# RWKV stage of a decoder layer on one core: TensorE's order laid down by a counted clock over generators, the 16x16 inverses started one half ahead

## The chip, the cores and the metric

One NeuronCore of a Trainium2 chip runs the whole program. The metric is the device time of one execution in microseconds; the time before is the median of three runs, 2283.53 us (2280.61 to 2289.46).

## What is computed

One decoder layer over 1024 tokens of width 1024, all in float32: token mixing (RWKV-7 time mixing, sparse attention and two sigmoid gates, from one input projection), then memory cross-attention, then a gated MLP with a width-3 convolution. The change lies in the RWKV part alone:

```python
def step(state, inp):
    r_t, w_t, k_t, v_t, a_t, b_t = inp
    sa = jnp.einsum('bhvk,bhk->bhv', state, a_t)
    state = (state * w_t[:, :, None, :] + sa[..., None] * b_t[:, :, None, :]
             + v_t[..., None] * k_t[:, :, None, :])
    return state, jnp.einsum('bhvk,bhk->bhv', state, r_t)
```

Eight heads of 64 channels each carry a 64x64 state over 1024 steps. `a` is minus the normalised key and `b` is that key times a learned rate, so each step erases along the key and writes anew.

## The kernel before, in words

The recurrence is computed in chunks of 64 steps. The stage handles **units**: a unit is a pair of heads (128 partitions) and one half of the sequence (512 steps, 8 chunks), and there are 8 of them. What follows is done for each unit by the generator `rwkv_half`, which stops at two `yield`s.

* **Operands.** Two small products of the low-rank projections (`pw`, `pa`, L564 and L566), decays by a scan (`CU`, L572) and exponentials, the key's norm (`inv_norm`: `vs` L540, then transposes `bc` L552), scaled keys `BH`, `KH`, `BB`, `KB`.
* **Couplings.** For each chunk the 64x64 products `gb` (L615) and `gk` (L621), masked to triangles by VectorE into `GB` (L616) and `AMR` (L625); transposes `tr` (L630) into `KS`, `SV`, `ZV`; the bonus term `pbo` (L597).
* **Substitution.** The strictly lower triangle `LT` (a half of `GB`) has to be inverted as 1 - L. Its 16x16 diagonal blocks go out to DRAM and back in another layout (`d1`, L653; `LB`, L655), VectorE inverts them in 30 short rows (L662, L663), GpSimd copies (L664), and they return through DRAM (`d2`, L665) into `DD` and `EE` by 16 DMAs on SP's queue (L674).
* **Inverse.** Five groups of small matmuls combine 16x16 blocks to 64x64: `q` (L680), `d` (L686), `e` (L693), `q` (L700), `e` (L708), each with a VectorE or ScalarE step behind it.
* **Recurrence.** Per chunk three matmuls that depend on one another: `x` (L719), copied to `XS` by VectorE (L721); `sa` (L723), copied to `SV` by VectorE and ScalarE (L724, L725); `z` (L728), added to the decayed state `ZV` by VectorE (L731).
* **Outputs.** `psy` from `AMR` and `ZV` (L735) and from `GB` and `SV` (L738), a group norm by `inv_norm`, scale and bonus, one DMA to `ya` (L749).

Beside the units there is wide work, 128x128 weights against 512 columns, three matmuls to a product (`mm3`, L193 to L195): the projections `prj` that feed the units (13 of them, 48 matmuls each), and the merge gates `gt`. The gates belong to no unit: 16 column blocks of 48 matmuls, 768 in all, made by the generator `gate_parts` one k step (three matmuls) at a time. They are due only when the branches are merged, far behind.

What sets the order of the work: the scheduler of the framework places each engine's instructions by the order in which the code names them and by a priority. The code names a unit's first part two units ahead (`pre`), the recurrence of a unit and the inverse of the next with high priority, and after that a chunk of gates (16 k steps) as often as `GATES1` says:

```python
for i in range(8):
    with tc.high_priority(offset=100000):
        next(its[i], None)
        if i < 7:
            next(its[i + 1])
    if i < 6:
        pre(i + 2)
    for _ in range(GATES1[i]):
        gate_chunk()
```

The attention stage that follows first issues `gate_chunk(GT)` (8 k steps), loads keys and values (`kld`, `vld` on GpSimd's queue, transposes `kT` L808), and then runs key blocks (`weights`, `values`; the first matmul of a block's values is L944). At each block `fill` takes about one step of the generator `fillers`: what is left of the gates, then the products of the merge (`mg`), the second part of which waits until the upper half of the attention is stored.

Of the kernel before, what the change touches and what calls it, by code (L numbers as in the profile page):

```python
# [18 lines left out]
P = 128  # L19
# [29 lines left out]
XQ = 3  # L49
LC, LS = (2, 2)  # L50
# [73 lines left out]
def layer_kernel(ctx: ExitStack, tc, I, out, cst):  # L124
# [384 lines left out]
    def k4(name, dt=F32):  # L509
        return rp.tile([P, NC8, 2, CH], dt, tag="k4", name=name, bufs=8)  # L510
# [25 lines left out]
    def inv_norm(sq, bank_, tile_, scale, eps):  # L536
# [12 lines left out]
        S.activation(w.rearrange("p (a d) -> p a d", d=64), rs[:, :, None].to_broadcast([P, 8, 64]), AF.Copy)  # L549
        ps = bank_("bc")  # L550
# [6 lines left out]
    def rwkv_half(hp, half, X):  # L557
        Xr, Xk, Xv = X
# [12 lines left out]
        r8 = lambda a: a.rearrange("p (c t) -> p c t", t=CH)  # L571
# [4 lines left out]
        S.activation(E3, E3, AF.Exp, scale=-DEC)  # L576

        TMP, KKN = e2("TMP"), e2("KKN")
        S.activation(TMP, Xk, AF.Square, scale=pc("rwkv_k_k", hp))
        ps = inv_norm(TMP, pss, ew, 64.0, None)  # L580
# [5 lines left out]
        V.tensor_tensor(BH, BH, E2, op=OP.mult)  # L586
        V.tensor_tensor(KH, KP, E2, op=OP.mult)
# [6 lines left out]
        TMP, BV = e2("TMP2"), ec("BV")  # L594
        V.scalar_tensor_tensor(TMP, Xr, pc("rwkv_r_k", hp), KP, op0=OP.mult, op1=OP.mult)
        ps = pss("pbo")
        PE.matmul(ps, ones, TMP, start=True, stop=True)  # L597
        V.scalar_tensor_tensor(BV, ps, 64.0, Xv, op0=OP.mult, op1=OP.mult)

        AMR = k8("AMR")  # L600
        for h, rw in enumerate(rows_h):
            V.scalar_tensor_tensor(AMR[rw, :, 0, h, :], r8(KKN[rw]), -1.0, r8(E3[rw]), op0=OP.mult, op1=OP.mult)
            V.tensor_tensor(AMR[rw, :, 1, h, :], r8(Xr[rw]), r8(ET[rw]), op=OP.mult)

        GB, KS, SV, ZV = k4("GB"), k4("KS"), k4("SV"), k4("ZV")
        zvs[hp, half] = ZV
        if half == 0:
            for h, rw in enumerate(rows_h):
                G.memset(ZV[rw, 0, h, :], 0.0)
        for j in range(2):  # L610
            ps = pss("gb").rearrange("p (c a t) -> p c a t", a=2, t=CH)
            for ci in range(4):
                c = 4 * j + ci
                for h, rw in enumerate(rows_h):
                    PE.matmul(ps[rw, ci], BH[rw, c * CH:(c + 1) * CH], AMR[rw, c, :, h, :], start=True, stop=True)  # L615
            V.tensor_tensor(GB[:, 4 * j:4 * j + 4].rearrange("p c a t -> p c (a t)"), ps.rearrange("p c a t -> p c (a t)"), bc(gmask, 4), op=OP.mult)  # L616
            ps = pss("gk").rearrange("p (c a t) -> p c a t", a=2, t=CH)
            for ci in range(4):
                c = 4 * j + ci
                for h, rw in enumerate(rows_h):  # L620
                    PE.matmul(ps[rows_h[1 - h], ci], KH[rw, c * CH:(c + 1) * CH], AMR[rw, c, :, h, :], start=True, stop=True)  # L621
            for h in range(2):
                rx = rows_h[1 - h]
                m = gmask[rx].rearrange("p (a t) -> p a t", a=2)[:, None].to_broadcast([64, 4, 2, CH])
                V.tensor_tensor(AMR[rx, 4 * j:4 * j + 4, :, h, :], ps[rx], m, op=OP.mult)  # L625

        for src, flip, dsts in ((BB, 0, (KS,)), (KB_, 1, (KS,)), (Xv, 1, (ZV, SV))):
            ps = pss("tr").rearrange("p (c n) -> p c n", n=P)
            for c in range(4):
                PE.transpose(ps[:, c, :], src[:, c * P:(c + 1) * P], ident)  # L630
            if src is Xv:

                mv = sm.tile([P, 4, 2], F32, name="vm", tag="vm", bufs=2)
                V.tensor_reduce(mv, ps.rearrange("p c (h d) -> p c h d", h=2), axis=AX.X, op=OP.add)
            for q, rq in enumerate(rows_h):
                for h in range(2):
                    ro = rows_h[1 - h] if flip else rows_h[h]
                    for dst in dsts:
                        o, i = dst[ro, q:NC8:2, h, :], ps[rq, :, h * 64:h * 64 + 64]
                        if src is Xv:  # L640
                            m = mv[rq, :, h][:, :, None].to_broadcast([64, 4, 64])
                            V.scalar_tensor_tensor(o, m, -1.0 / 64, i, op0=OP.mult, op1=OP.add)
                        else:
                            S.activation(o, i, AF.Copy)


        LT = GB[:, :, 0, :]
# [16 lines left out]
        G.tensor_copy(DB[:, 1], DB[:, 0].rearrange("p a b -> p b a"))  # L664
        SP.dma_start(d2.rearrange("w a c s t -> (a c) w (s t)"), DB.rearrange("p w s t -> p w (s t)"))  # L665
        UU, DD, EE = r8(et("UU")), r8(et("DD")), kd("EE")
        QQ = UU
        G.memset(DD, 0.0)
        G.memset(EE, 0.0)
        for hb in range(8):  # L670
# [103 lines left out]
    for i in range(8):  # L774
# [4 lines left out]
        if i < 6:  # L779
            pre(i + 2)  # L780
# [577 lines left out]
```

## Time and profile before

| what | time |
|---|---|
| median of 3 runs | 2283.53 us |
| the profiled execution | 2278.23 us |
| its span | 2276.5 us |
| TensorE busy | 2197.2 us |
| RWKV stage, 212 to 757 us of the span | 545 us |
| up to the first value block of the attention, 757 to 798 us | 41 us |
| attention, 798 to 1150 us | 352 us |

The span is the time from the first to the last instruction of the trace; the profiled execution's own time is 1.7 us more. A busy time counts a matmul from its start to its modelled end, so that in a dense stretch each overlaps the next.

### The profile page before, as it was taken

Reading aid. Unit: us, or ns where it says so; the run is one execution under the profiler, and the core shown is the slowest. Engines: PE = TensorE matmul, PEld = TensorE weight load, DVE = VectorE, ACT = ScalarE, POOL = GpSimd, SP = SyncE. Lnnn points to the kernel's source line nnn. Section 1 sums busy time; section 2 is a strip of 40 time slices with the busy share of each in tenths; the row PEclk is TensorE's granted clock in tenths of the full one; section 3 lists DMA queues with packets and bytes.
Section 4 is the critical chain, followed back from the end, with each engine's and each line's share of the span. In section 5 each row is a group of like instructions: output and inputs, shape, how many; then the busy total and the mean of one; then the engine's idle time right before and its main releaser. Section 6 shows DMA issues by size and latency. Waiting matters only on the chain.

```text
span 2276.5 us, 33702 instructions
## 1 busy us (share of the span) xinstructions
PE 2197.2 (97%) x13252; PEld 1777.9 (78%) x13252; DVE 1273.3 (56%) x2503; ACT 872.1 (38%) x1434; POOL 453.8 (20%) x512
## 2 busy tenths in 40 slices
PE   8999999999999899999989999999999999999998
PEld 7989766667667667677679988898888888888886
DVE  4332475868674487878873735366443434444447
ACT  3342333433432466766741434134222313222232
POOL 1222121212220044444450201020010101000013
PEclk9999999999999999999999999999999999999999
DMA  6354111111122401212153412102111111112102
GB/s 206 114 154 140 42 39 41 40 48 33 40 55 60 122 29 31 77 56 66 56 168 115 149 38 93 56 29 65 47 47 47 47 54 40 56 47 65 51 33 83
DMA packets 197931, 158.03 MB, mean 69 GB/s; under 512 B 49301, under 2 KB 173198, under 8 KB 197774
## 3 DMA queue, kind: packets, MB, share of 16 engines
q1 hardware_dynamic: 186062, 139.11, 20.0%
q10 hardware_dynamic: 11136, 14.68, 1.9%
q8 instruction: 105, 1.72, 0.3%
q0 software_dynamic: 576, 2.10, 0.3%
q14 instruction: 52, 0.43, 0.1%
HBM read 125.86 MB, written 29.98 MB: 68 GB/s over the span
## 4 chain that ended last, share of the span: by engine, by line
PE 82%; DVE 9%; ACT 3%; DMA 3%; issue 2%; POOL 1%; SPq 0%; DVEq 0%; ACTq 0%; POOLq 0%
PE up L195 7%; PE up L193 7%; PE up L194 7%; PE dn L193 4%; PE dn L195 4%; PE dn L194 4%; PE op L193 2%; PE op L194 2%; PE op L195 2%; PE gt L195 2%; PE gt L193 2%; PE gt L194 2%; PE prj L195 2%; PE prj L194 2%; PE np L193 2%
## 5 line engine op out<-in xcount | busy, mean ns | idle before, releaser
L199 DVE TENSOR_TENSOR wl<-raw,wh 128x1024 fp32r<-128x1024 f32 (+1 forms) x164 | 204.0, 1244 | 276.0 <-ACT wh L198 275.5
L198 ACT ACTIVATE wh<-raw 128x1024 fp32r<-128x1024 f32 (+1 forms) x164 | 173.0, 1055 | 463.7 <-PE dn L195 137.5
L193 PE MATMUL up<-nTh,wh 128*128 128x512 f32 x704 | 276.6, 393 | 0.0
L194 PE MATMUL up<-nTl,wh 128*128 128x512 f32 x704 | 276.4, 393 | 0.0
L195 PE MATMUL up<-nTh,wl 128*128 128x512 f32 x704 | 276.2, 392 | 0.0
L1283 DVE SCALAR_TENSOR_TENSOR cv<-up,pv,cv 128x511 f32<-128x511 f32 (+1 forms) x176 | 131.5, 747 | 148.7 <-ACT cv L1281 147.0
L1307 POOL TENSOR_TENSOR cv<-cv 128x512 f32<-128x512 f32 x44 | 56.9, 1292 | 630.9 <-DVE cl L1287 413.6
L195 PEld LDWEIGHTS up<-nTh,wl 128*128 128x128 f32 x704 | 132.2, 188 | 29.8
L194 PEld LDWEIGHTS up<-nTl,wh 128*128 128x128 f32 x704 | 132.2, 188 | 29.7
L193 PEld LDWEIGHTS up<-nTh,wh 128*128 128x128 f32 x704 | 132.2, 188 | 29.5
L929 POOL TENSOR_TENSOR pl<-pe,ph 128x512 fp32r<-128x512 f32 x87 | 115.1, 1329 | 163.7 <-ACT ph L928 130.0
L193 PE MATMUL dn<-wh,gT 128*128 128x512 f32 x352 | 138.2, 393 | 0.0
L195 PE MATMUL dn<-wh,gT 128*128 128x512 f32 x352 | 137.6, 391 | 0.0
L194 PE MATMUL dn<-wl,gT 128*128 128x512 f32 x352 | 136.8, 389 | 0.0
L1318 DVE SCALAR_TENSOR_TENSOR acc<-acc,dn 128x512 f32<-128x512 f32 x96 | 65.5, 686 | 95.4 <-PE dn L195 94.8
L1281 ACT ACTIVATE cv<-up,pv 128x512 f32<-128x512 f32 x88 | 68.6, 779 | 119.6 <-PE up L195 119.6
L193 PE MATMUL gt<-xTh,wh 128*128 128x512 f32 x256 | 106.6, 417 | 2.4 <-ACT gst L469 1.8
L195 PE MATMUL gt<-xTh,wl 128*128 128x512 f32 x256 | 107.2, 419 | 0.0
L194 PE MATMUL gt<-xTl,wh 128*128 128x512 f32 x256 | 107.0, 418 | 0.0
L193 PE MATMUL np<-wh,xTh 128*128 128x256 f32 (+1 forms) x320 | 92.1, 289 | 1.6 <-ACT wh L198 1.6
L1158 POOL TENSOR_TENSOR acc<-acc,lngb 128x1024 f32<-128x1024 f32 x21 | 50.4, 2398 | 207.8 <-DVE mv L1153 136.1
L195 PE MATMUL np<-wh,xTl 128*128 128x256 f32 (+1 forms) x320 | 91.5, 287 | 0.0
(357 smaller groups left out, 5576.1 us busy)
## 6 DMA issues: line engine op xcount, KB each, us to landing
raw<-in_ffn_w_up_dram SPq DMA_DIRECT2D x88, 256.0 KB
raw<-in_w_in_dram SPq DMA_DIRECT2D x37, 512.0 KB
raw<-in_ffn_w_down_dram SPq DMA_DIRECT2D x22, 512.0 KB
gscr<-gst ACTq DMA_DIRECT2D x32, 256.0 KB
xt<-in_x_dram SPq DMA_DIRECT2D x8, 512.0 KB
rawn<-nst SPq DMA_DIRECT2D x32, 128.0 KB
raw<-in_xa_wk_dram SPq DMA_DIRECT2D x8, 512.0 KB
raw<-in_xa_wv_dram SPq DMA_DIRECT2D x8, 512.0 KB
```

Source lines behind the costliest of these rows:

```text
L193: PE.matmul(o, lh, rh, start=start, stop=False)
L194: PE.matmul(o, lh, rl, start=False, stop=False)
L195: PE.matmul(o, ll, rh, start=False, stop=stop)
L198: S.activation(h, src, AF.Copy)
L199: V.tensor_sub(l, src, h.bitcast(F32))
L929: in_turn("l", LTURN)(l, e, h.bitcast(F32), op=OP.subtract)
L1158: (V if tt == NT - 1 else G).tensor_tensor(r[:, c], r[:, c], gb[:, 1, c], op=OP.add)
L1281: S.activation(c, ps, AF.Identity, scale=pc("cw2", ci), bias=pc("ffn_conv_b", ci))
L1283: V.scalar_tensor_tensor(c[:, s:], ps[:, :HALF - s], pc(nme, ci), c[:, s:], op0=OP.mult, op1=OP.add)
L1307: G.tensor_tensor(c[0], c[0], c[1], op=OP.mult)
L1318: V.scalar_tensor_tensor(v, v, 1.0 if f else ALPHA, ps, op0=OP.mult, op1=OP.add)
```

## The change

`rwkv_half` is split into five generators for each unit: `operands`, `couplings`, `inverse`, `recurrence`, `outputs`. Each `yield a, b` says how long the matmuls just named take TensorE (`a`, us) and how long after that the next part can't begin (`b`, us). A loop keeps a clock: it takes, in a fixed order of classes, the first task that is due, lets it name its next matmuls, and advances the clock by `a`. Projections and gates are tasks too, three matmuls (one k step, counted as 0.69 us) at a time; the gates come last, whenever nothing else is due. TensorE's order is then exactly the order of naming (`manual_schedule`); the other engines are scheduled as before.

The product that gives `LT` is taken out of `gb` and becomes `gl`, 64x64, named as soon as its two operands are there and before the other couplings; `gb` is now 64x64 too. The inverse may begin when the clock stands 36 us after `gl` (`L_SUBST`), and is done while the recurrence of the unit before it runs. The outputs of a unit are named in one piece behind its recurrence. `-KKN*E3` is made once into `E3` by VectorE and copied to `AMR` by ScalarE, where VectorE made it twice. `k4` goes from 8 to 6 buffers, `GB` and `LT` have two of their own. `GATES1` is no longer used; the lines of the attention stage are the same.

```diff
+L_DENSE = 0.69
+L_SUBST = 36
+L_BACK = 7
...
     def k4(name, dt=F32):
-        return rp.tile([P, NC8, 2, CH], dt, tag="k4", name=name, bufs=8)
+        return rp.tile([P, NC8, 2, CH], dt, tag="k4", name=name, bufs=6)
+
+    def k2(name):
+        return rp.tile([P, NC8, CH], F32, tag=name, name=name, bufs=2)
...
             ps = pg("prj")
-            gemmT(ps, w, cc, xT, half)
-            shifted(ps, dsts[half], idx, half, last)
+            for k in range(8):
+                mm3(ps, *w.at(k, cc, P), *xT.mov(k, half), k == 0, k == 7)
+                if k == 7:
+                    shifted(ps, dsts[half], idx, half, last)
+                yield L_DENSE, 0, k < 7
...
         V.tensor_tensor(BH, BH, E2, op=OP.mult)
+        V.scalar_tensor_tensor(E3, KKN, -1.0, E3, op0=OP.mult, op1=OP.mult)
         V.tensor_tensor(KH, KP, E2, op=OP.mult)
...
+        u.operands = Xr, E3, ET, BH, KH, BB, KB_, TMP
+        u.WC = WC
+        yield 0.5, 6.0
+
+        ps = pss("gl").rearrange("p (c t) -> p c t", t=CH)
+        for c in range(NC8):
+            for rw in rows_h:
+                cs = slice(c * CH, (c + 1) * CH)
+                PE.matmul(ps[rw, c], BH[rw, cs], E3[rw, cs], start=True, stop=True)
+        LT = k2("LT")
+        V.tensor_tensor(LT, ps, bc(gmask[:, 0:CH], NC8), op=OP.mult)
+        u.LT = LT
+        start = clock[0]
+        yield 1.2, 0.5
...
         SP.dma_start(d2.rearrange("w a c s t -> (a c) w (s t)"), DB.rearrange("p w s t -> p w (s t)"))
+        while me and not inverses[me - 1].done or me > 1 and not recurrences[me - 2].done:
+            yield 0, 0.5
         UU, DD, EE = r8(et("UU")), r8(et("DD")), kd("EE")
...
         G.tensor_tensor(UU, LT, bc(csr[:, C_M16:C_M16 + 64], NC8), op=OP.mult)
-        yield
+        u.UU, u.DD, u.EE, u.due = UU, DD, EE, max(start + L_SUBST, clock[0] + L_BACK)
...
+    def couplings(me):
...
+        for h, rw in enumerate(rows_h):
+            V.tensor_tensor(AMR[rw, :, 1, h, :], r8(Xr[rw]), r8(ET[rw]), op=OP.mult)
+            S.activation(AMR[rw, :, 0, h, :], r8(E3[rw]), AF.Copy)
...
+        yield 0, 3.0
+        ps = pss("gb").rearrange("p (c t) -> p c t", t=CH)
+        for c in range(NC8):
+            for h, rw in enumerate(rows_h):
+                PE.matmul(ps[rw, c], BH[rw, c * CH:(c + 1) * CH], AMR[rw, c, 1, h, :], start=True, stop=True)
+        V.tensor_tensor(GB, ps, bc(gmask[:, CH:P], NC8), op=OP.mult)
...
+    def inverse(i):
...
         S.activation(QQ, ps, AF.Copy)
+        yield 0.8, 1.2
...
+    def recurrence(i):
...
             V.tensor_copy(XS, ps[:, 0:P])
+            yield 0.3, 1.1
...
             S.activation(SV[64:128, c, 1, :], ps[64:128, 64:128], AF.Copy)
+            yield 0.3, 1.3
...
+                yield 0.3, 1.7
+
+    def outputs(i):
+        u, (hp, half) = units[i], divmod(i, 2)
+        AMR, GB, SV, ZV = u.AMR, u.GB, u.SV, u.ZV
         psy = pso("psy")
...
+        def ready(self):
+            if not self.started:
+                self.started = self.may()
+                self.due = max(self.due, clock[0])
+            return self.started and self.due <= clock[0]
+
+        def step(self):
+            with tc.high_priority(offset=100000) if self.urgent else ExitStack():
+                r = next(self.gen, None)
+            if r is None:
+                self.done = True
+            else:
+                clock[0] += r[0]
+                self.due = clock[0] + r[1]
+                self.open = len(r) > 2 and r[2]
...
+    operands_ = [Task(operands(i), (lambda i=i: first.done if i == 0 else couplings_[i - 1].done)) for i in range(8)]
+    couplings_ = [Task(couplings(i), (lambda i=i: hasattr(units[i], "WC") and projections[i // 2 * 3 + 2].done and (i < 2 or hasattr(units[i - 2], "out")))) for i in range(8)]
+    inverses = [Task(inverse(i), (lambda i=i: clock[0] >= getattr(units[i], "due", 1e9)), True) for i in range(8)]
+    recurrences = [Task(recurrence(i), (lambda i=i: inverses[i].done and couplings_[i].done), True) for i in range(8)]
+    outputs_ = [Task(outputs(i), (lambda i=i: recurrences[i].done)) for i in range(8)]
+    wide = Task(gates_timed())
+    dense = (first, *projections)
+    classes = (recurrences, outputs_, inverses, couplings_, operands_, dense, [wide])
+    with tc.manual_schedule(engines={mybir.EngineType.PE}):
+        while not all(t.done for t in outputs_):
+            for tasks in classes:
+                t = next((t for t in tasks if not t.done), None)
+                if tasks is dense and wide.open:
+                    continue
+                if t is not None and t.ready():
+                    t.step()
+                    break
+            else:
+                clock[0] += 0.25
```

**TensorE, before: a chunk of a recurrence (unit 2) among the gates.** The product `psy` stands right behind the state that it reads, on both sides of `x`.

```order
L735 MATMUL psy<-AMR,ZV 64x64
L194 MATMUL gt<-xTl_87,wh 128x512
L719 MATMUL x<-ZV,AMR 128x128
L735 MATMUL psy<-AMR,ZV 64x64
L195 MATMUL gt<-xTh_85,wl 128x512
L193 MATMUL gt<-xTh_85,wh 128x512
L194 MATMUL gt<-xTl_87,wh 128x512
L723 MATMUL sa<-XS,EE 128x128
L195 MATMUL gt<-xTh_85,wl 128x512
L193 MATMUL gt<-xTh_86,wh 128x512
L194 MATMUL gt<-xTl_88,wh 128x512
L728 MATMUL z<-SV,KS 128x128
```

**TensorE, changed: a chunk of a recurrence (unit 3) among the projections.**

```order
L783 MATMUL x<-ZV,AMR 128x128
L196 MATMUL prj<-xTh_81,wh 128x512
L197 MATMUL prj<-xTl_83,wh 128x512
L198 MATMUL prj<-xTh_81,wl 128x512
L196 MATMUL prj<-xTh_81,wh 128x512
L197 MATMUL prj<-xTl_83,wh 128x512
L198 MATMUL prj<-xTh_81,wl 128x512
L788 MATMUL sa<-XS,EE 128x128
L632 MATMUL gl<-E_5498,BH 64x64 x16
L196 MATMUL prj<-xTh_81,wh 128x512
L197 MATMUL prj<-xTl_83,wh 128x512
L198 MATMUL prj<-xTh_81,wl 128x512
```

The chunk keeps its three matmuls, with whole groups of three wide ones between them (`gl` is unit 5's), and `psy` is gone from it: all 32 of a unit stand behind its recurrence.

**TensorE, changed: where the inverse of unit 4 begins.** `q` reads `DD`, which comes back from DRAM; before, it was cut into pieces of 1 and 2 among gates, chunk steps and `psy`.

```order
L788 MATMUL sa<-XS,EE 128x128
L728 MATMUL pbo<-TMP_4983,csr 128x512
L739 MATMUL q_5472<-DD,UU 64x64 x16
L794 MATMUL z<-SV,KS 128x128
L583 MATMUL pw<-LO,lw 128x512
L585 MATMUL pa<-LO,lw 128x512
L746 MATMUL d_5512<-UU,EE 32x32 x16
L783 MATMUL x<-ZV,AMR 128x128
```

Now all 16 stand in one piece, ahead of a `z` of unit 3's recurrence and of the first matmuls of unit 5.

**VectorE, changed: from unit 4's triangle to its substitution** (`stmp` and `DB`; `XS`, `SV`, `ZV` are those of unit 2's recurrence).

```order
L634 TENSOR_TENSOR LT<-gl,csr 128x512
L789 COPY SV<-sa 64x64
L799 SCALAR_TENSOR_TENSOR ZV<-ZV,WC,z 64x64 x2
L785 COPY XS<-x 128x128
L202 TENSOR_TENSOR wl<-raw,wh 128x1024
L789 COPY SV<-sa 64x64
L529 SCALAR_TENSOR_TENSOR X_4924<-prj,pv,X_4924 128x511
L799 SCALAR_TENSOR_TENSOR ZV<-ZV,WC,z 64x64 x2
L654 TENSOR_TENSOR stmp<-DB,LB 64x1
```

The first row of the substitution, which reads `LB` from DRAM, stands eight entries behind the triangle; behind it come the next copies of the recurrence.

## Rows read from the trace of the kernel before

**Rows 1.** The page: span, and the busy time of the engines.

```profile
span 2276.5 us, 33702 instructions
PE 2197.2 (97%) x13252; PEld 1777.9 (78%) x13252; DVE 1273.3 (56%) x2503; ACT 872.1 (38%) x1434; POOL 453.8 (20%) x512
```

**Rows 2.** Busy time in two windows: us, engines' busy us (instructions), clock, DMA share, GB/s.

```profile
212.00:757.00 545.00, 524.55 (x4177) 382.32 (x4176) 348.54 (x852) 195.02 (x358) 102.61 (x119) 1.00 0.18 46
757.00:798.00 41.00, 34.88 (x146) 27.41 (x144) 21.04 (x33) 20.90 (x32) 4.96 (x5) 0.92 0.56 162
```

**Rows 3.** Waits of TensorE's weight loads, 212 to 757 us: us, times, longest.

```profile
PEld psy L735 <- DVE ZV L731: 19.7, 51, 0.9
PEld z L728 <- ACT SV L725: 16.1, 39, 2.1
...
PEld pa L566 <- ACT E L567: 0.2, 1, 0.2
```

**Rows 4.** Timeline, TensorE: first and last of 37 wide matmuls in a row.

```profile
763.65 0.39 PE L195 MATMUL gt<-xTh,wl 128*128 128x512 f32 x1
...
771.81 0.39 PE L195 MATMUL gt<-xTh,wl 128*128 128x512 f32 x1
```

**Rows 5.** The gates (tile gt) alone, by window: us, PE, PEld, ACT busy.

```profile
212.00:757.00 545.00, 164.39 (x536) 90.29 (x536) 12.55 (x21) 1.00 0.18 46
757.00:798.00 41.00, 29.90 (x113) 22.26 (x112) 3.26 (x6) 0.92 0.56 162
798.00:1150.00 352.00, 35.57 (x120) 21.52 (x120) 3.28 (x6) 1.00 0.18 54
```

**Rows 6.** Attention: line L944, one matmul for each block, in two windows.

```profile
820.00:860.00 40.00, 8.82 (x22) 3.04 (x22) 1.00 0.00 1
940.00:1140.00 200.00, 32.78 (x80) 11.11 (x80) 1.00 0.21 63
```

**Rows 7.** The same windows, line L195: a third of the filler's matmuls.

```profile
820.00:860.00 40.00, 1.17 (x3) 0.56 (x3) 1.00 0.00 1
940.00:1140.00 200.00, 32.33 (x81) 15.23 (x81) 1.00 0.21 63
```

**Rows 8.** Timeline of a chunk of unit 2's recurrence: start, us, engine.

```profile
407.20 0.38 PE L723 MATMUL sa<-XS,EE 128*128 128x128 f32 x2
...
407.87 0.22 ACT L725 ACTIVATE SV<-sa 64x64 f32<-64x64 f32 x1 [1.95 <-DVE SV L724]
...
408.15 0.49 PE L728 MATMUL z<-SV,KS 128*128 128x128 f32 x2
408.67 0.59 DVE L731 SCALAR_TENSOR_TENSOR ZV<-ZV,WC,z 64x64 f32<-64x64 f32 x2
```

**Rows 9.** Timeline of unit 7's substitution, from its triangle to the last DMA back.

```profile
663.88 0.67 DVE L616 TENSOR_TENSOR GB<-gb,csr 128x512 f32<-128x512 f32 x1
...
674.44 0.15 DVE L662 TENSOR_TENSOR stmp<-DB,LB 64x1 f32<-64x1 f32 x1
...
689.43 0.37 DVE L663 TENSOR_REDUCE DB<-stmp 64x15 f32<-64x225 f32 x1
...
690.60 0.62 SPq L665 DMA_DIRECT2D d<-DB  x1
...
693.43 0.33 SPq L674 DMA_DIRECT2D DD<-d  x1
...
701.68 0.43 SPq L674 DMA_DIRECT2D EE<-d  x1
```

**Rows 10.** Timeline, unit 6: its triangle, its last DMA to DD, its first products.

```profile
619.82 0.68 DVE L616 TENSOR_TENSOR GB<-gb,csr 128x512 f32<-128x512 f32 x1
...
661.95 0.43 SPq L674 DMA_DIRECT2D DD<-d  x1
...
666.36 1.14 PE L680 MATMUL q<-DD,UU 64*64 64x64 f32 x30
```

**Rows 11.** Timeline ahead of the attention: keys asked for, and their transposes.

```profile
760.72 1.07 POOL L802 DMA_DIRECT2D kld<-rawn  x1
...
772.04 1.03 PE L808 MATMUL kT<-ident,kld 128*128 128x128 f32 x8
```

More of the change, by code (lines that the diff above doesn't have):

```diff
@@ L576, in rwkv_half @@
         S.activation(E3, E3, AF.Exp, scale=-DEC)
+        yield 1.3, 0.5
+        while not projections[3 * hp].done:
+            yield 0, 0.5
+        Xk = Xs[hp, 1][half]
         TMP, KKN = e2("TMP"), e2("KKN")
         S.activation(TMP, Xk, AF.Square, scale=pc("rwkv_k_k", hp))
-        ps = inv_norm(TMP, pss, ew, 64.0, None)
+        w = norm_sums(TMP, pss, ew, 64.0, None)
+        yield 1.0, 4.5
+        while not projections[3 * hp + 1].done:
+            yield 0, 0.5
+        Xr = Xs[hp, 0][half]
+        ps = norm_back(w, pss)
         V.scalar_tensor_tensor(KKN, Xk, pc("rwkv_k_k", hp), ps, op0=OP.mult, op1=OP.mult)
@@ L756, in piece @@
         return wload([wc_(a)]), 0
-    project(*piece(3 * RC), 12, [LO[:, 0:HALF], LO[:, HALF:T]])
-    S.activation(LO[0:64, :], LO[0:64, :], AF.Tanh)
-    Xs, its = {}, {}
-    def pre(i):
-        hp, half = divmod(i, 2)
-        if half == 0:
-            Xs[hp] = [[ex(f"X{a}{j}") for j in range(3)] for a in range(2)]
-            for j in range(3):
-                project(*piece(j * RC + hp * P), j * 4 + hp, [Xs[hp][a][j] for a in range(2)])
-        its[i] = rwkv_half(hp, half, Xs[hp][half])
-        next(its[i])
@@ L771, in layer_kernel, with __init__ @@
-    pre(0)
-    pre(1)
-    next(its[0])
-    for i in range(8):
-        with tc.high_priority(offset=100000):
-            next(its[i], None)
-            if i < 7:
-                next(its[i + 1])
-        if i < 6:
-            pre(i + 2)
-        for _ in range(GATES1[i]):
-            gate_chunk()
+    clock = [0.0]
+    units = [Half() for _ in range(8)]
+    Xs = {}
+    class Task:
+        def __init__(self, gen, may=lambda: True, urgent=False):
+            self.gen, self.may, self.urgent, self.started, self.done, self.due, self.open = gen, may, urgent, False, False, 0.0, False
+        def ready(self):
[12 more added lines that the diff above has]
+                self.open = len(r) > 2 and r[2]
@@ new lines, in decays, with projected, may_project @@
+    def decays():
+        yield from project(*piece(3 * RC), 12, [LO[:, 0:HALF], LO[:, HALF:T]])
+        S.activation(LO[0:64, :], LO[0:64, :], AF.Tanh)
+    def projected(hp, j):
+        Xs[hp, j] = [ex(f"X{a}{j}") for a in range(2)]
+        yield from project(*piece(j * RC + hp * P), j * 4 + hp, Xs[hp, j])
+    def may_project(hp, j):
+        if hp == 0:
+            return first.done
+        return couplings_[2 * hp - 1].done if j == 2 else couplings_[2 * hp - 2].done and hasattr(units[2 * hp - 1], "WC")
```

141 lines of the change are left out of this document (82 added, 59 removed).

## The prediction

> **What bounds the kernel now.** I read the page first: TensorE is busy in 97% of the span [rows 1]. That alone would say that only its work counts. Then I took the stage that the change touches, from the first projection at 212 us to 757 us, with the busy time by window: 524.55 of 545 us [rows 2]. So by busy time TensorE idles 545 - 524.55 = 20.5 us there. The third view says otherwise: in the same stretch the weight loads waited 103 us, in 51 rows, of which the first, second and last are shown; the largest are `psy` for `ZV`, 19.7 us, and `z` for `SV`, 16.1 us [rows 3]. Both are right. A wide matmul counts as busy for 390 ns, and the next one starts 227 ns after it (36 steps from 763.65 to 771.81, so 8.16/36) [rows 4]; each time that a small matmul has to wait behind a wide one, some 160 ns of the wait look busy. The Trainium skill, page "Trainium Kernel Development and Optimization", section "Performance Expectations", says so too: matmul busy time is a bad measure of how near a kernel is to its bound, the weight loads' is a good one. By busy time the stage could gain 20 us at the most; by the weight loads' waits, about 100. I work with the second.
>
> So of the stage's 545 us some 442 are work: the wide matmuls, 624 of the projections and 536 of the gates [rows 5], 1160 x 0.227 = 263 us, and the small ones, 179 us, 22 a unit. 103 are waits, each too short to fill a slice of the page.
>
> **The change, part by part.** *More gates in the stage.* The laid-down order has 691 gate matmuls ahead of the last norm of the stage, where 536 are now. 155 x 0.227 = +35 us of work in the stage, and as much less behind it.
>
> *The split of `gb`.* 64x64 against 64x128: 16 products a unit become 32 of half the width. A run of 30 `q` records, which have the form of `gl`, takes 1.14 us [rows 10]; `gl` adds 32 such records a unit, and `gb` gets shorter. Between 0 and 8 x 1.2 = 10 us; I take +5. VectorE's and ScalarE's share of the new `E3` changes hands off the path.
>
> *Waits that have no place any more.* `psy` now stands behind the recurrence, so its 19.7 us go. In the recurrence the clock leaves 0.3 + 1.3 = 1.6 us from `sa` to `z` and 0.3 + 1.7 = 2.0 us from `z` to `x`. In the trace `sa` starts at 407.20 and ScalarE has `SV` at 407.87 + 0.22, so 0.89 us; `z` starts at 408.15 and `ZV` is done at 408.67 + 0.59, so 1.11 us [rows 8]. Wide groups of 0.68 us fill the difference, so most of the 16.1 us of `z` go as well. Of the 103 us I leave 25: waits of short latency at changes between small and wide matmuls, and a copy now and then behind a long row of VectorE. Bounds: 10, if only the latencies are left, and 60, if the other engines' queues are as late as now.
>
> *A wait that the change adds.* `q` of a unit reads `DD`, and TensorE, which takes its matmuls in order, now meets all 16 of them in one piece about 36 us of its own work behind `gl`. For unit 4 the new order has 90 wide matmuls between the two, 90 x 0.227 = 20.4 us, and of the unit's 22 us of small ones about 15 (the inverse, two or three chunk steps and the first products of the next unit lie outside): 35.5 us. The other units have 78 to 87 wide ones and a chunk step or the norm's products more; I take 36 for all. How long the data needs is in the trace: in unit 7 the triangle is masked at 663.88 + 0.67, the substitution's first row runs at 674.44, its last ends at 689.80, `d2` is issued at 690.60, the first of 16 DMAs to `DD` and `EE` at 693.43 and the last is issued by 702.11 [rows 9]. That is 9.9 + 15.4 + 3.6 + 8.7 = 37.6 us. For the landing there is an upper bound: in unit 6 the last DMA to `DD` is issued by 662.38 and `q` runs at 666.36, 4.0 us [rows 10]; I take 2.5. `gl` itself and its mask cost 2 us ahead of that (1.14 and 0.67, with a change of engine). Sum: 37.6 + 2.5 + 2 = 42 us. One microsecond comes off because the new order of VectorE has on average that much less foreign work between the first and the last row of the substitution. So 41 us are needed where TensorE has 36 to do: 5 us of waiting. The windows of units 0 and 1 overlap and share one wait, so 7 x 5 = +35 us. What waits behind `q`: the recurrence's next `z`, the next unit's `pw` and `pa`, and all gates; nothing of it can pass. Bounds: 38.5 us (the landing at 1 us, the substitution 1.5 us shorter) gives 7 x 2.5 = 17; unit 6's whole way, 666.36 - 620.50 = 45.9 us, and 2 us for `gl`, with the parts that now have less in the queue taken off, 46 us, gives 7 x 10 = 70.
>
> Stage: 442 + 35 + 5 + 35 + 25 = 542 us, 3 less than now.
>
> *Behind the stage.* From 757 to 798 us the loads of keys, their transposes and the first scores form a chain, covered by 113 gate matmuls, 25.7 us [rows 5]; the new order has 74 up to the first value block. The chain doesn't get longer for that: the keys are asked for at 760.72 and their transposes stand in line behind gates until 772.04 [rows 11]. It can get shorter by some of these 11 us; I take 2. That most of the 39 gates' time is not won here is the price of having them earlier: TensorE idles instead. The granted clock, 0.92 in this window [rows 2], can fall further with less work; I leave that in the range.
>
> In the attention the order has 75 gate and merge matmuls fewer between the first and last value matmul, 17 us; twice the second half of the merge is not yet allowed and the generator is stepped in vain. Does TensorE's time there go down with them? From 820 to 860 us there were almost no fillers: 22 blocks in 40 us, 1.82 us each; from 940 to 1140 us, 80 blocks in 200 us, 2.50 us each [rows 6]. Fillers: 3 x 3 and 3 x 81 matmuls [rows 7], so 0.09 and 0.69 us a block. 0.60 us less filler made a block 0.68 us shorter: the stretch is TensorE's, and what is taken away is won. I take 15 of 17 us.
>
> **Sum:** -3 - 2 - 15 = -20 us. From the profiled execution's 2278.23 us that is 2258; the median of the runs shown is 5.3 us higher, so I forecast 2264 us.
>
> **The rivals.** *The wait at `q` doesn't come.* VectorE has as few as five foreign entries between unit 4's substitution rows in the new order, and the landing may be short; then the 35 us go: stage 507, and 2278 - 38 - 17 = 2223, 2229 as a median. For it: the slack of 5 us is small against legs that differ by 4 from unit to unit. Against: the 37.6 us of unit 7 were among the shortest.
>
> *The substitution sets the pace* (the other sign). VectorE takes its rows in order. The first row of the substitution waits for `LB`, 9.9 us behind the triangle; the new order puts eight entries there, some 5 us of work, and the next `XS` and `SV` stand behind it, so the recurrence waits too, and each unit's way stretches to 46 us. Price: 7 x 10 = 70 in place of 35, stage 577, 2278 + 32 - 17 = 2293, 2299 as a median. It turns the sign by over 0.5% once the way is over 45 us, at an added wait of 9 us a unit. For it: unit 6's 45.9 us. Against: that unit had an output's DMA and other rows in between. The Trainium skill, page "TensorE: Matmul & The Clock Gate", section "Architectural detail", states that VectorE and ScalarE are strict queues while TensorE can pull weight loads ahead; by that rule nothing behind the waiting row can go around it, which is this rival; the order of the rows in the trace shows no exception.
>
> *What is taken from behind the stage is not won.* If the attention is as long without its 75 fillers, because VectorE, not TensorE, sets it, and the chain ahead of it stays, only the 3 us of the stage are left: 2281. Against it stand the two windows of rows 6.
>
> **How the numbers follow.** My forecast 0.40, no wait at `q` 0.22, nothing won behind the stage 0.20, the substitution sets the pace 0.18. A measurement of this kernel can tell about 0.5%, 11 us, from no change. Faster by more: most of the first case (0.36) and the second: 0.58. Within: 0.04 and the third: 0.24. Slower: 0.18. The forecast's own range is 2250 to 2280 (the wait at 38.5 or 44 us). For 8 in 10 I go down to the second case with 5 us of its smaller waits gone too, 2224, and up to the pace rival, 2300.
>
> **What would show it.** Right: the stage ends near 212 + 542 = 754 us of the new span with 690 gates done, `psy` in TensorE's waits is gone, `q` or the matmuls just behind it show a wait for the DMAs to `DD` of some 35 us in all, and from the stage's end to the first value block TensorE's busy share falls while the time stays near 40 us. Wrong: a stage under 515 us (the added wait isn't there), or over 570 with the waits at `XS`, `SV` or `q`; or an attention that is as long as now with 75 matmuls fewer.

## The result, and the profile after

The changed kernel takes 2305.67 us (median of 4 runs, 2304.18 to 2307.25) against 2286.03 of the kernel before (4 runs beside them): ratio 1.0088, 95% interval 1.0064 to 1.0112. It is slower by 0.9%, where I had forecast 0.9% faster; the time lies outside my range. The profiled execution took 2305.22 us, 27.0 more than the 2278.23 from which the sum was made.

The page of the changed kernel, where [rows 1] stood:

```profile
span 2303.4 us, 34187 instructions
PE 2175.1 (94%) x13508; PEld 1788.7 (78%) x13508; DVE 1256.4 (55%) x2495; ACT 897.4 (39%) x1462; POOL 445.9 (19%) x512
```

TensorE has 256 matmuls more and is busy 22 us less, in a span 27 us longer. Where the time is, three windows of each kernel tell: from the stage's first projection to its last transposes `bc`, from there to the first value matmul, and from there to the first matmul of the output projection. First before, then changed (us; busy us and instructions of PE, PEld, DVE, ACT, POOL; granted clock; DMA share; GB/s):

```profile
212.10:757.10 545.00, 524.55 (x4177) 382.27 (x4176) 348.63 (x852) 195.12 (x358) 102.61 (x119) 1.00 0.18 46
757.10:810.90 53.80, 47.03 (x203) 37.01 (x202) 32.50 (x57) 24.65 (x38) 4.96 (x5) 0.94 0.51 151
810.90:1184.80 373.90, 358.32 (x1750) 255.57 (x1750) 302.48 (x611) 253.37 (x443) 175.37 (x145) 1.00 0.20 63
```

```profile
214.10:790.50 576.40, 525.34 (x4588) 419.36 (x4587) 336.06 (x847) 228.66 (x395) 98.73 (x119) 0.93 0.20 51
790.50:840.60 50.10, 32.87 (x139) 24.67 (x137) 30.59 (x56) 20.47 (x32) 4.92 (x5) 0.86 0.40 110
840.60:1211.30 370.70, 348.63 (x1661) 241.52 (x1660) 298.23 (x608) 249.76 (x439) 171.97 (x145) 0.97 0.20 60
```

The stage is 31.4 us longer, the stretch behind it 3.7 shorter, the attention 3.2 shorter; the stage begins 2 us later and the rest is as long as it was. So the loss is the stage's. And its clock, 1.00 before [rows 2], is 0.93. In stretches (same columns):

```profile
212.00:300.00 88.00, 75.28 (x401) 58.47 (x400) 42.07 (x84) 32.60 (x49) 15.45 (x22) 0.89 0.21 55
300.00:400.00 100.00, 91.07 (x912) 72.75 (x911) 68.35 (x170) 36.37 (x66) 19.25 (x24) 0.96 0.19 43
400.00:500.00 100.00, 88.92 (x850) 70.35 (x848) 66.51 (x177) 43.32 (x75) 22.52 (x25) 0.95 0.16 39
500.00:600.00 100.00, 89.17 (x862) 70.17 (x861) 62.61 (x161) 46.33 (x82) 17.77 (x25) 0.88 0.16 39
600.00:700.00 100.00, 93.20 (x901) 75.24 (x900) 67.51 (x180) 40.42 (x73) 21.18 (x23) 0.93 0.21 53
700.00:790.00 90.00, 89.29 (x687) 74.12 (x686) 30.09 (x79) 29.80 (x53) 2.56 (x2) 1.00 0.26 77
```

Length times (1 - clock), summed, is 9.7 + 4 + 5 + 12 + 7 + 0 = 37.7 us: with the two levels of 2.4 and 1.2 GHz that is 75 us at half clock. If the trace's clock records are laid over the waits of the weight loads, 26 of these 75 us lie inside waits, where TensorE's next product had to wait anyway, and 49 lie in work.

The waits of the weight loads in the stage, where [rows 3] stood (us, times, longest):

```profile
PEld vs L549 <- ACT TMP L601: 19.4, 6, 4.9
PEld pa L585 <- issue: 14.5, 4, 6.5
PEld z L794 <- ACT SV L790: 8.7, 15, 1.3
...
PEld pw L583 <- ACT LO L863: 4.5, 1, 4.5
...
PEld q L739 <- issue: 1.7, 5, 0.8
```

`psy`, 19.7 us in 51 waits before, is gone, as the change intends. In its place stand few and long ones: `vs` 6 times, up to 4.9 us, `pa` 4 times, up to 6.5. Neither was among the large waits before; `pa` had next to nothing [rows 3], and `vs` this:

```profile
PEld vs L540 <- ACT TMP L579: 2.5, 4, 0.7
```

Summed over all rows of the view, the stage has 97 us of waits in 101 pieces, where it had 103 us in 235. So the waits didn't go; they became fewer and longer.

What happens at the longest of them, in unit 1 (here cut to the rows that matter), the timelines of TensorE, VectorE and ScalarE show (start, us, engine; idle time and its releaser in brackets):

```profile
281.86 1.12 PE L583 MATMUL pw<-LO,lw 64*128 64x512 f32 x2
288.69 2.04 PE L585 MATMUL pa<-LO,lw 64*128 64x512 f32 x2 [5.71 <-DVE SV L719]
...
291.25 0.63 PE L197 MATMUL gt<-xTl,wh 128*128 128x512 f32 x1
291.68 0.63 PE L198 MATMUL gt<-xTh,wl 128*128 128x512 f32 x1
295.20 1.86 PE L549 MATMUL vs<-csr,TMP 128*128 128x2 f32 x8 [2.89 <-ACT TMP L601]
```

```profile
287.10 0.42 DVE L719 SCALAR_TENSOR_TENSOR ZV<-vm,tr 64x256 f32<-64x256 f32 x1
287.55 0.53 DVE L654 TENSOR_TENSOR stmp<-DB,LB 64x225 f32<-64x225 f32 x1
288.12 0.42 DVE L719 SCALAR_TENSOR_TENSOR SV<-vm,tr 64x256 f32<-64x256 f32 x1
```

```profile
290.82 0.69 ACT L588 ACTIVATE AG<-pa,hbias 128x512 f32<-128x512 f32 x1 [7.12 <-PE pa L585]
...
293.90 0.63 ACT L594 ACTIVATE E<-E 128x512 f32<-128x512 f32 x1 [1.36 <-POOL E L593]
294.44 0.71 ACT L601 ACTIVATE TMP<-X,pv 128x512 f32<-128x512 f32 x1
```

`pa` takes the PSUM bank that the eight copies of `Xv`'s transposes to `ZV` and `SV` have to leave; VectorE makes them in turn with rows of the substitution. `vs` needs `TMP`, which asks for nothing but a projection that was done long before, but stands in ScalarE's queue behind `AG` (which waits for `pa`) and three exponentials, one of which waits for POOL. The counted clock knows neither: it leaves 0.5 us between `pa` and `vs`. Three windows around it:

```profile
270.00:282.00 12.00, 12.00 (x109) 9.35 (x108) 9.34 (x31) 4.91 (x10) 0.00 (x0) 1.00 0.25 72
282.00:290.00 8.00, 2.29 (x4) 0.65 (x4) 7.59 (x19) 0.69 (x1) 1.22 (x2) 0.65 0.00 0
290.00:302.00 12.00, 9.11 (x25) 6.58 (x25) 3.52 (x5) 7.87 (x12) 3.24 (x5) 0.52 0.23 43
```

TensorE was busy without a break at 1.00, then 2.29 of 8 us, and the clock is 0.52 in the twelve us behind that: a wide matmul there starts 0.43 us after the one ahead (291.25 to 291.68), not 0.227 as in [rows 4].

### The profile page after: what moved, and what is told of

Read it like the earlier page. It is cut to its first block, busy times and chain, and to the rows that moved or that the text cites. A ratio compares the mean times of both kernels' runs of the same rounds, so it can differ in the third digit from the quotient of the medians.

```text
span 2303.4 us, 34187 instructions
## 1 busy us (share of the span) xinstructions
PE 2175.1 (94%) x13508; PEld 1788.7 (78%) x13508; DVE 1256.4 (55%) x2495; ACT 897.4 (39%) x1462; POOL 445.9 (19%) x512
## 4 chain that ended last, share of the span: by engine, by line
PE 77%; DVE 10%; DMA 5%; ACT 3%; issue 3%; POOL 1%; SPq 1%; ACTq 0%; DVEq 0%; POOLq 0%
PE up L198 7%; PE up L196 7%; PE up L197 7%; PE dn L196 4%; PE dn L198 4%; PE dn L197 3%; PE op L196 2%; PE op L198 2%; PE op L197 2%; PE gt L196 2%; PE gt L197 2%; PE gt L198 2%; PE prj L196 2%; PE prj L197 2%; DVE wl L202 2%
## 5 line engine op out<-in xcount | busy, mean ns | idle before, releaser
L196 PE MATMUL gt<-xTh,wh 128*128 128x512 f32 x256 | 114.9, 449 | 8.1 <-ACT gst L472 8.1
L196 PE MATMUL prj<-xTh,wh 128*128 128x512 f32 x208 | 91.9, 442 | 1.6 <-ACT wh L201 1.6
L1043 ACT ACTIVATE ph<-pe 128x512 fp32r<-128x512 f32 (+1 forms) x148 | 89.7, 627 | 6.6 <-POOL macc L1161 4.6
```

The costliest lines, as they stand in the source:

```text
L196: PE.matmul(o, lh, rh, start=start, stop=False)
L1043: S.activation(h, e, AF.Copy)
```

## The experiments

Theory A: the loss is these long waits, and the half clock behind them. Its rivals are those I had named, the substitution's pace (B) and no gain behind the stage (C), and, from the fifth run on, that a wait taken away always comes back elsewhere (D). All medians and stages follow; "waits" is the sum of the weight loads' waits in the stage. The kernel before has a stage of 545.0 us, a clock of 1.00 and 103 us of waits; each ratio is to runs of it made beside that kernel.

| kernel | median us | ratio to before, 95% | stage us | its clock | waits us |
|---|---|---|---|---|---|
| changed | 2305.67 | 1.0088 (1.0064 to 1.0112) | 576.4 | 0.93 | 97 |
| 1 later `vs` | 2306.68 | 1.0095 (1.0073 to 1.0116) | 584.6 | 0.94 | 104 |
| 2 later `vs`, `pw` and `pa` | 2320.52 | 1.0158 (1.0135 to 1.0182) | 592.7 | 0.95 | 106 |
| 3 waits filled | 2304.62 | 1.0084 (1.0061 to 1.0106) | 573.8 | 0.97 | 71 |
| 4 substitution given 46 us | 2323.92 | 1.0172 (1.0148 to 1.0197) | 596.6 | 0.92 | 101 |
| 5 `TMP` earlier | 2274.75 | 0.9972 (0.9955 to 0.9990) | 546.7 | 0.96 | 72 |
| 6 and `pbo` earlier | 2263.64 | 0.9921 (0.9906 to 0.9936) | 542.3 | 0.96 | 70 |
| 7 gates held back | 2304.23 | 1.0099 (1.0084 to 1.0115) | 563.6 | 0.91 | 113 |
| 8 both of 6, some gates held back | 2269.31 | 0.9949 (0.9932 to 0.9965) | 534.4 | 0.96 | 79 |
| 9 as 6, later `vs` | 2284.51 | 1.0007 (0.9996 to 1.0019) | 548.2 | 0.96 | 78 |
| 10 as 6, substitution given 28 us | 2344.77 | 1.0268 (1.0253 to 1.0284) | 609.9 | 0.91 | 133 |
| 11 as 6, `Xv` first | 2260.07 | 0.9906 (0.9886 to 0.9925) | 537.0 | 0.97 | 72 |
| 12 as 11, substitution given 39 us | 2270.54 | 0.9947 (0.9930 to 0.9964) | 545.9 | 0.98 | 86 |

**1 and 2: the steps put later.**

```diff
-        yield 1.3, 0.5
+        yield 1.3, 9.0
```

and for the second, ahead of `pw`, `yield 0, 5.0 if me else 0` besides.

> The changed kernel, with the clock of the operands telling 9.0 in place of 0.5 us between the two decay products (pw, pa) and the norm's sums (vs). Everything else is laid down by the same rules; the counted clock's end moves from 493.8 to 498.0 us, with 6 more gate steps (18 matmuls, 4.1 us) in the stage. Theory A (long single waits of TensorE, and the half clock that follows them): the waits of vs for TMP, 19.4 us in 6 in the changed kernel, fall under 4 us, the stretches at half clock in the stage, 75 us, shorten to 30 to 50 us, the stage goes from 577 us to 545 to 560, the median from 2306 to 2280 to 2290. Theory B (the substitution's way to DD sets the pace): the operands come later, so the substitution too; the stage is as long or longer, 2306 to 2320. Theory C (the loss lies behind the stage, in the chain up to the first value block): within 5 us of 2306.

> The same, and 5 us of the counted clock between the release of a unit's operands and its pw and pa, for all units but the first, so that pa's bank has been read by the copies to SV and ZV. Counted clock's end 504.2 us, 15 more gate steps than the changed kernel (10.2 us of work moved into the stage). Theory A: the waits of vs and of pa, 19.4 and 12.8 us, fall under 4 us each, half clock in the stage under 25 us in place of 75; the stage, with the 10 us of moved work, 535 to 555 us in place of 577; 2270 to 2285. Theory B: as long or longer, 2306 to 2320. Theory C: some 10 us less behind the stage by the moved gates at most, 2296 to 2306.

Both go against Theory A. Their times, 2306.7 and 2320.5 us, are about what B had said (2306 to 2320), the first also what C had said. In the first `vs` is gone from the list and others have grown; in the second `pa` has nearly gone too, and the projections wait for their weights and `q` for its data in its place. The largest in the first and in the second:

```profile
PEld pa L585 <- issue: 28.7, 6, 7.1
PEld sa L788 <- DVE XS L785: 14.1, 14, 1.8
```

```profile
PEld prj L198 <- DVE wl L202: 12.4, 5, 6.2
PEld q L739 <- issue: 12.1, 6, 3.7
```

A later step moves all that is laid down behind it, so these two changed more than the wait. The waits in sum are no fewer (104 and 106 us, 97 in the changed kernel), which speaks for D, or for a bad experiment. Run 4 tests B, run 5 tests D.

**3: the waits filled.** Useless products ahead of `pw`, and 12 of the same ahead of `vs`, into the banks that these then overwrite:

```diff
+        for b in range(8 if me else 0):
+            PE.matmul(ps, xT.mov(0, 0)[0][:, 0:P], xT.mov(0, 0)[0], start=True, stop=True)
```

> The changed kernel with useless wide matmuls where TensorE waits longest: 12 ahead of each vs, into the bank that vs then overwrites, and 8 ahead of each pw, in units 1 to 7: 140 x 0.227 = 32 us of work that computes nothing. The order is otherwise the same. If the waits cost only themselves: the added work lies in waits of 32 us at the most and spills over by some microseconds where a wait is shorter than its filling: 2306 to 2316, and the half clock in the stage still 60 us or more. If the half clock is what follows the long waits and costs on its own: half clock in the stage under 40 us in place of 75, and the kernel gets faster in spite of the work, 2285 to 2300.

140 useless matmuls, 31.8 us of them, and the kernel is no slower. The stage, and its two waits:

```profile
214.30:788.10 573.80, 543.58 (x4728) 437.22 (x4727) 335.98 (x847) 229.23 (x395) 100.70 (x119) 0.97 0.20 51
```

```profile
PEld vs L551 <- ACT TMP L605: 9.1, 5, 2.4
...
PEld pa L589 <- issue: 5.4, 3, 4.5
```

The waits at `vs` and `pa` in these rows fall from 33.9 to 14.5 us; all waits of the stage together fall by 25.7, from 97.0 to 71.3. What is left of the stage without its waits, the work, goes from 479.4 to 502.5 us: 23.1 more, though 31.8 were put in. So 8.7 us of work came back, and the clock is what changed: the time at half clock falls from 75 to 38 us, and the part of it that lies in work from 49.0 to 31.4. The clock fell out as the second case said. The time, 2304.62, meets neither case; it shows that the useless work cost nothing. The Trainium skill, page "TensorE: Matmul & The Clock Gate", section "HAM oscillation — how this bites in real kernels", prices time at half clock at one half of its length. 8.7 us for the 17.6 us of work at half clock that went is 0.49, so the trace agrees for work; for all the 37.6 us that went it is 0.23, since 20 of them had lain in waits.

**4: ten us more for the substitution** (`L_SUBST = 46`).

> The changed kernel with 46 in place of 36 us of the counted clock between the gl products and the inverse's first product, 11 more gate steps (7.5 us) in the stage. Theory A: the inverse's first product waited only 1.7 us in all, so nothing is won there; 2300 to 2312, with the waits at vs and pa as before. Theory B: the substitution's way is what TensorE's long waits come from; with 10 us more for it they go, 2270 to 2290.

18 us slower. B had this 15 to 35 us faster: it falls. Theory A's "nothing" was wrong as well. All steps have shifted, and `vs` waits more, as the listing of this run says:

```profile
PEld vs L549 <- ACT TMP L601: 30.0, 7, 5.1
```

**5 and 6: the waits' causes taken away, and TensorE's order left as it is.** `TMP` is asked for ahead of `pw`; then `pbo` stands ahead of the last transposes, so that the three banks turn differently and `pa` gets one that a single row leaves:

```diff
+        while not projections[3 * hp].done:
+            yield 0, 0.5
+        S.activation(TMP, Xk, AF.Square, scale=pc("rwkv_k_k", hp))
         ps = pss("pw")
...
-        S.activation(TMP, Xk, AF.Square, scale=pc("rwkv_k_k", hp))
         w = norm_sums(TMP, pss, ew, 64.0, None)
```

```diff
         for src, flip, dsts in ((BB, 0, (KS,)), (KB_, 1, (KS,)), (Xv, 1, (ZV, SV))):
+            if src is Xv:
+                ps = pss("pbo")
+                PE.matmul(ps, ones, TMP, start=True, stop=True)
```

> The changed kernel with ScalarE's square TMP, which vs waits for, asked for ahead of pw and pa in place of behind the five steps of the decay that follow them. TensorE's order stays what it is but for unit 0, whose pw and pa come one projection half later. Theory A (long single waits, and the half clock behind them, are the loss): the waits of vs, 19.4 us, and of pw for LO, 4.5 us, go; half clock in the stage 35 to 55 us in place of 75; 2275 to 2290. Theory D (something else sets the stage's pace, and a wait that is taken away comes back at another place, as the later vs of the first two runs suggest): other waits grow by about as much as these fall; 2300 to 2310.

> The same, and the product pbo put ahead of the last of a unit's three groups of transposes, so that the turn of the three banks gives pa the bank that pbo leaves after one row of VectorE, and not the one that the eight copies to SV and ZV leave; 4 gate steps fewer in the stage. Theory A: the waits of pa, 12.8 us, go as well; half clock under 30 us; 2260 to 2280. Theory D: 2300 to 2310, with waits grown elsewhere.

One row of ScalarE asked for earlier takes 31 us out (26 by the two ratios, each against its own runs of before), and turns the change from slower to a little faster than the kernel before; the second edit takes 11 more. The stage of run 5:

```profile
212.20:758.90 546.70, 514.86 (x4588) 414.40 (x4587) 336.12 (x847) 229.28 (x395) 99.99 (x119) 0.96 0.21 53
```

It has the same 4588 matmuls as in the changed kernel and is 29.7 us shorter. 25 us of that are waits (97 to 72 in sum; 19.4 at `vs` and 4.5 at `pw` are gone), so nothing came back at others. The remaining 4.5 us are work, of which 36 us lie at half clock in place of 49. D falls here: what it predicted, 2300 to 2310, did not come.

Run 6 is another matter. `pa` waits no longer, but `vs` now waits 12 us for the bank, and the sum of the waits stays (72 and 70 us), as D has it; the half clock is 41 us, not under 30. Its stage is 4.4 us shorter, 3.0 of them for 13 gate matmuls that left it; the stretch behind it and the attention are 3.4 and 3.0 us shorter. So the 11 us are measured, but that they come from the waits at `pa` is not shown.

**7 and 8: gates held back.** The changed kernel and run 6, with `return` in the gates' generator after 176 and 200 steps.

> The changed kernel with no more than 176 gate steps (528 matmuls, 536 before the change) in the stage; 163 gate matmuls, 37 us, go to the stretches behind it: 27 to the one up to the first value block, 136 to the attention. If TensorE's work sets the time at both places: the stage 540 us, what is behind it 37 us longer, 2304 to 2310. If the gates are hidden behind the stage (my rival that nothing was won there): 2270 to 2285. If the stage's pace is a chain of waits and not TensorE's work (Theory D): the stage stays over 560 us, the time goes up to 2310 to 2335.

> The square ahead of pw, pbo ahead of the last transposes, and no more than 200 gate steps (600 matmuls) in the stage; 24 more gate matmuls up to the first value block and 67 more in the attention than in the changed kernel. Theory A, with gates hidden behind the stage: 2250 to 2268, faster than both kernels. Theory A alone: 2260 to 2280. Theory D: 2295 to 2315.

Run 7, stage and attention:

```profile
213.60:777.20 563.60, 500.07 (x4427) 397.33 (x4426) 331.85 (x844) 222.19 (x386) 98.92 (x119) 0.91 0.18 46
...
823.90:1209.20 385.30, 369.84 (x1799) 264.45 (x1798) 304.93 (x612) 258.01 (x446) 174.94 (x145) 1.00 0.21 64
```

163 matmuls, 37 us, less shorten the stage by 12.8; 136 more, 30.9 us, lengthen the attention by 14.6. At both places a gate matmul costs less than half of its time, since it fills waits: without them the stage's waits grow from 97 to 113 us, with them the attention's fall from 67 to 49. The time is that of the first case in the expectation, the stage (over 560 us) that of the third. The sum is nil: the place of the gates doesn't explain the loss, and C is no cause of it. Run 8 comes out as Theory A alone had it (2260 to 2280) and is 6 us slower than run 6: its stage is 8 us shorter, its attention 10 longer.

**9 and 10: what a wait covers, and what `q` really needs.** Run 6 with `yield 1.3, 3.0` between `pa` and `vs`, and with `L_SUBST = 28`.

> The version with the square ahead of pw and pbo ahead of the last transposes (2264 us), with 3.0 in place of 0.5 us of the counted clock between pa and vs: vs there still waits 12.1 us for the bank that the copies to SV and ZV leave. 3 gate steps fewer in the stage. Theory A: the 12 us of waits go and no other grows by as much; half clock a little under the 41 us of that version; 2250 to 2262. Theory D: 2260 to 2270.

> The same version (2264 us) with 28 in place of 36 us of the counted clock between gl and the inverse's first product q, 11 gate steps (7.5 us) fewer in the stage. My prediction took 41 us as what the data of q needs after gl. Then q would wait some 13 us a unit, 6 units or more, and the time be over 2320. The traces of the changed kernel and of this version show the last DMA to DD issued 30 to 35 us after gl, so 31 to 36 with its landing: then q waits 2 to 8 us in each of six or seven units, 15 to 40 us in all, with half clock behind it; 2265 to 2290.

Run 9 misses both: 21 us slower than run 6. `vs` waits 2.8 us now, but `q` waits for `DD`, 14.7 us in the two rows below and 3.3 in run 6. The stretch behind the stage is 5 us longer, the attention 7:

```profile
PEld q L740 <- DMA DD<-d: 8.3, 3, 3.6
...
PEld q L740 <- issue: 6.4, 5, 3.4
```

The attention has 28 gate matmuls, 6.4 us, that run 6 had done ahead of it; why the stretch before it got longer was not followed further. Run 10 shows my term at `q` as a thing by itself:

```profile
PEld q L740 <- issue: 56.8, 15, 8.0
```

```profile
595.47 0.45 PE L740 MATMUL q<-DD,UU 64*64 64x64 f32 x2 [7.36 <-DMA DD<-d]
599.38 1.94 PE L740 MATMUL q<-DD,UU 64*64 64x64 f32 x30 [3.46 <-DMA DD<-d]
```

The waits, some 8 us a unit in seven, lie between the two expectations, the time is that of the first: the stage is 68 us longer than in run 6, 63 of them waits, and the clock went down to 0.91. (The 30 to 35 us in that expectation were read too short: in units 1 to 7 of the changed kernel the last of the 16 DMAs is issued 33 to 39 us after `gl`.) So the mechanism is real, and its edge is near the 36 us of the change: 8 us less cost 81.

**11 and 12: the last long wait.** Run 6 with the transposes of `Xv` first of the three and `pbo` between the two others, so that `vs` gets the bank that ScalarE's copies leave; then with `L_SUBST = 39`.

> The version with the square ahead of pw and pbo ahead of the last transposes (2264 us), with the transposes of Xv, which VectorE copies to SV and ZV, first of the three groups in place of last, and pbo between the two others, so that vs gets the bank that ScalarE's copies to KS leave. TensorE's order is otherwise the same, gates and all. Theory A: the 12.1 us of vs for that bank go, with some half clock behind them; 2248 to 2262. Theory D (the wait comes back elsewhere, as q's wait for DD did when vs was put later): 2260 to 2272.

> The same with 39 in place of 36 us of the counted clock between gl and q, 3 gate steps (2 us) more in the stage. If the waits that went had covered the way of DD, as in the run with the later vs, q waits in the version with 36 and no longer here: some 5 to 10 us faster than that one. If 36 is enough, the two are within 6 us of each other.

```profile
215.70:752.70 537.00, 502.58 (x4575) 405.27 (x4574) 337.66 (x847) 228.76 (x395) 97.72 (x119) 0.97 0.21 53
...
800.60:1166.80 366.20, 344.65 (x1657) 239.50 (x1657) 297.56 (x607) 247.54 (x435) 176.17 (x145) 0.98 0.20 59
```

```profile
PEld tr L716 <- issue: 11.5, 7, 2.2
```

These are run 11's windows of the stage and the attention, and its largest wait. The waits for a bank move to the next transposes, 11.5 us in 7 of at most 2.2, and the waits in sum stay at 72 us, as D has it; 2260.07 lies in the ranges of both theories. The stage is 5 us shorter all the same: now 23 us of its work lie at half clock, in place of 34. Run 11 is the fastest, 0.9% under the kernel before, but run 6 is within its interval. Run 12 is 10 us slower and meets neither expectation: `q` had little left to gain (no wait of its own among the large ones of run 11), and the stage's other waits grow by 14 us, most of all at the inverse's second `q` (L763, 11.2 us).

## Why the prediction was wrong

**The step that failed: "Of the 103 us I leave 25".** The stage kept 97 us of waits, 95 of them not at the `q` that I gave a term of its own. I checked the counted clock against the trace at two places, the recurrence and the way of `DD`, and took the rest as short latencies. The operands' own `yield 1.3, 0.5` I didn't check, though the diff has it: it puts `vs` 0.5 us of TensorE's time behind `pa`. `vs`, `pa` and `pw` alone wait 38.4 us. Run 5, which takes the cause of two of them away and leaves nearly all of TensorE's order as it is, has 25 us fewer of waits and is 31 us faster: that much is shown, not argued. The rest of the term was too small as well: even runs 6 and 11 keep 70 and 72 us of waits, and no run tells how much of those comes from `AMR`'s copies, now on ScalarE, or from the fewer buffers of `k4`.

**The clock, "I leave that in the range".** I spoke of it for the stretch behind the stage only. In the stage it went from 1.00 to 0.93. 103 us of short waits left it at 1.00 [rows 2, 3]; 97 us in fewer and longer ones didn't. Of the 49 us of work at half clock some 23 are lost, an estimate from the spacing of the wide matmuls, 0.43 us there and 0.227 in [rows 4]; run 3, with 17.6 us less of such work and 8.7 us won, bears it out.

**How the terms add up.** The stage is 97 us of waits and 479 of work, where I had 25 + 35 = 60 and 442 + 35 + 5 = 482. So the waits are all that my sum lacks, and the work looks right; but it is so by luck. 23 of the 479 us are the clock's, so at full clock it is about 456, some 26 less than I had. What is left to explain it are the small products, since at full clock one wide product starts 0.23 us after another in both kernels (median in the stage). Which of them got cheaper, no run tells; the 5 us for the split of `gb` were not measured by themselves.

**"I take 36 for all", "41 us are needed": the wait at `q`, +35 us, is not there.** In unit 7 of the changed kernel (rows of three engines, those between left out):

```profile
670.60 1.09 PE L632 MATMUL gl<-E,BH 64*64 64x64 f32 x30
671.80 0.69 DVE L634 TENSOR_TENSOR LT<-gl,csr 128x512 f32<-128x512 f32 x1 [0.80 <-PE gl L632]
681.83 0.15 DVE L654 TENSOR_TENSOR stmp<-DB,LB 64x1 f32<-64x1 f32 x1 [1.92 <-DMA LB<-d]
694.19 0.37 DVE L655 TENSOR_REDUCE DB<-stmp 64x15 f32<-64x225 f32 x1
697.74 0.33 SPq L667 DMA_DIRECT2D DD<-d  x1
704.28 0.43 SPq L667 DMA_DIRECT2D DD<-d  x1
706.07 1.19 PE L739 MATMUL q<-DD,UU 64*64 64x64 f32 x32
```

TensorE comes to `q` 35.5 us after `gl`, near the 36 that I had counted as work alone (3.2 of them are waits here), and its data is there. `gl` and its mask take 1.9 us, the way to the first row 9.3 (9.9 predicted), the rows 12.7 (15.4 [rows 9]), the way to the first of the 16 DMAs 3.2 (3.6), from there to the last for `DD` 6.5; in run 10 `q` went on 2.0 us after that one was issued (597.36 to 599.38). Sum: 35.7 us, where I had 41. The difference lies in two legs, 2.7 us each: the rows, which differ by more than that from unit to unit, and the DMAs with their landing (8.5 us, 11.2 predicted), where I counted to the last DMA of `EE` and took an upper bound for the landing. In units 2, 3, 5 and 6 `q` came 38.8 to 43.9 us after `gl`, with 6 to 10 us of other waits in between. So the mechanism and one side were right, the other side was 5 us too long, and a difference of 5 between two such numbers was no ground for 35 us. Run 10 shows that with 8 us less the wait comes, run 9 that it comes when another goes. That `q` now stands in one piece changed little: in unit 6, 30 of its 32 products stood in one run before, too [rows 10].

**"+35" and "I take 15 of 17 us": the gates.** I booked them at full price where they came and where they left. Run 7 says 12.8 of 37 us in the stage, 14.6 of 30.9 in the attention. In the changed kernel the attention has 88 gate matmuls fewer (3 in place of 91), 20 us, and is only 3.2 us shorter: the weight loads' waits there grew by 18 us, from 49 to 67, and the clock fell from 1.00 to 0.97. So my reading of [rows 6], that less filler makes a block shorter by as much, did not hold here. The stretch behind the stage came as said, 3.7 us shorter (2 predicted), with TensorE's busy time down by 14.

**What held.** `psy` is gone, 691 gate matmuls stand in the stage (691 predicted), the chain behind the stage keeps its length, the weight loads' waits and not the busy time tell the stage's slack (TensorE is busy 525 us in the stage of both kernels, which differ by 31 us).

**The rivals.** The substitution's pace gave 2299, near the 2305.67 measured, by a way that is not there: run 4 gave it 10 us more and lost 18. No wait at `q` came true, and alone would have meant 2229: an error the other way that hid part of the first. That nothing is won behind the stage came true in the main, with 3.2 of 15 us in the attention, but by waits and clock; that VectorE sets the pace there is not shown. With the waits of `vs` and `pa` gone, run 11 stands at 2260, near the 2264 of my forecast, but not by its terms: the stage is 8 us shorter than before in place of 3, the stretch behind it 5.9 in place of 2, the attention 7.7 in place of 15.

**Two slips in the prediction's bounds.** A wait at 38.5 or 44 us a unit gives 7 x 2.5 less or 7 x 3 more, so 2246 to 2285 and not 2250 to 2280; and in the pace rival 9 us a unit make the kernel 8 us slower, 0.35% and not 0.5. Neither would have changed the outcome.

## What to carry to other kernels

An order laid down by a table of delays is only as good as its shortest delay: check every one of them against the trace, by the path of the data on all engines' queues and by the bank that the step will take, and not only those that the change speaks of. Many short waits can be cheaper than the few long ones that replace them: here TensorE's clock stayed at 1.00 through the former and not through the latter. Sum the waits before and after each edit, since a single wait that goes can come back under another name, as in runs 1, 6 and 11. Where a wait is long, ask first for the row that it waits for earlier; to put the waiting step later moves everything behind it.

## What the hardware showed

I had not expected that 140 useless matmuls, 31.8 us, could be added to the stage and leave it 2.6 us shorter, nor that some 23 us of the stage would be the clock's, in a stage where it had been 1.00, nor that about a third of the time at half clock, 26 of 75 us, would lie in waits. Nor had I expected how near the edge a laid-down order sits: 2.5 us of delay at one place (run 9) cost 21 us, and 8 us at another (run 10) 81.
